# A hybrid decoder layer on one core: modulation blocks loaded ahead of the first weights, and S5's products in turns on the two halves of the rows

## The chip, the core and the metric

One core of a Trainium2 chip runs the whole layer. The metric is the device time of one execution in microseconds (us), as the median of several runs. TensorE (PE, with PEld for its weight loads), VectorE (DVE), ScalarE (ACT), GpSimd (POOL) and SyncE (SP, which issues most of the DMAs) each work through a queue of their own in a fixed order; semaphores hold them back until what they need is there.

## What is computed

The reference takes `x` (1 x 1024 x 1024, float32) and a conditioning vector `c`, and gives an output of x's shape. Cut to what matters here:

```python
cond = silu(c)
mod = cond @ ada_w + ada_b
sh1, sc1, g1, sh2, sc2, g2 = split(mod, 6)
u = rmsnorm(h, norm_mix_w) * (1 + sc1) + sh1
proj = u @ w_in
...
bu = einsum('bsgh,gph->bsgp', ug, bb)
st = associative_scan(combine, (lam, bu))
y = einsum('bsgp,ghp->bsgh', st_re, c_re) - einsum('bsgp,ghp->bsgh', st_im, c_im) + d_skip * u
g = gelu(y)
y_d = g * sigmoid(g @ glu_w + glu_b)
...
h = h + g1 * (groups @ w_out)
v = rmsnorm(h, norm_mlp_w) * (1 + sc2) + sh2
h = h + g2 * (square(relu(v @ mlp_w1)) @ mlp_w2)
out = rmsnorm(h, final_norm_w)
```

The projection `proj` feeds four mixers: a causal pooling, a short gated convolution, an SSD (Mamba-2) and the S5 of the lines above, a state-space model with complex diagonal states in 16 groups.

## The kernel before, in words

The modulation is worked out by DVE, not by PE. The transposed `ada_w` lies in memory as 48 blocks of 128 x 1024, eight for each of the six parts (e = 0 is the shift `sh1`, 1 the scale `sc1`, 2 the gate `g1`, 3 and 4 the second shift and scale, 5 the second gate). `ada_load(e, k)` (L319) loads one, `ada_block` (L324, instruction at L326) multiplies it with the conditioning row and sums each row into a column of `mod`. `modulation` (L335) then makes the columns `amul` (L337) and `ash` (L339) for one block k of 128 input channels.

The input projection begins with the 768 columns that the SSD needs (L601 to L642). The rows of the sequence are taken in two halves h, and in each half k runs over the eight blocks of 128 input channels. In a step, `load_xw(k)` (L577) loads the weights and `split_xw` (L589, L590) splits them into a high part `wh` (on ACT) and a low part `wl` (on DVE), so that three products of the rounded kind make one exact enough. `modulated_T` (L359) transposes four blocks of normalised `x` on PE (L363), scales and shifts them with `amul` and `ash` on ACT (L365, the high part `uh`, and L368, the full one `t_u`) and takes the rest on DVE (L371, the low part `ul`, which it returns). Then 18 products (L638 to L640) add to six banks of PSUM. In the first half each step loads its weights, then two modulation blocks (e = 1 and 0), splits, sums the blocks and calls `modulation`. Before the second half, four more blocks of `x` are loaded (L100) and normalised (`ready`, L568: squares on ACT at L356, L347 and L348 on POOL, the scaling on DVE at L571). In the second half each step sums two more blocks (e = 2 and 4); their loads share three buffers (tag `g5`), while the first half's have four (`m`) and three (`g5`).

`s5_half(b)` (L463) is one half of S5, eight groups in four pairs q; the two groups of a pair, g2 = 0 and 1, lie on rows 0 to 63 and 64 to 127 of the states. After the scans on DVE it has `X[0]` and `X[1]`, the real and imaginary states before each chunk. For each g2 it takes a bank of PSUM, and for each q three products add to a quarter of it: the two states with their tables (L503, L504; 64 rows each, those of g2) and the inputs with a table `T` (L505, all 128 rows). These are plain float32 products, which the trace shows as two instructions each. The GELU follows for each bank on ACT and DVE (L508 to L512), then transposes (L519).

The order of every queue is written by a planner ahead of time. It goes through the program with a clock of its own, and gives each engine the first instruction in the program's order that its clock says is ready; `tc.high_priority()` puts the instructions within it ahead of the rest, and `tc.issue_after(i)` puts those within it behind `i` on i's engine. The chip then runs the queues in that order, whatever the real times are. The small tables of S5 (`s5_small`, L175) come first in the program and fill DVE's queue between other things. `ada_some` (L552) is called after the second half of S5 in program order, and sums eight blocks of e = 3 (`ws_ada`) on DVE, behind the last state of that half.

Of the kernel before, what the change touches and what calls it, by code (L numbers as in the profile page):

```python
# [21 lines left out]
P = 128  # L22
# [29 lines left out]
def body(ctx: ExitStack, tc: tile.TileContext, x, c, pk, adaT, w_x, w_zd, w_pl, w_gl, w_in, w_out, w1, w2, fnw, out):  # L52
    nc = tc.nc
    V, A, PE, G, SY = nc.vector, nc.scalar, nc.tensor, nc.gpsimd, nc.sync
# [14 lines left out]
    def bank(name, tag="ms"):  # L69
        return pp.tile([P, 512], F32, tag=tag, name=name)  # L70
# [25 lines left out]
    xt = [gran(f"x{tb}", tag="x") for tb in range(NB)]  # L96
# [212 lines left out]
    for h in range(2):  # L309
        ps = bank(f"cb{h}", "pj")  # L310
# [8 lines left out]
    def ada_load(s, j, tag="m"):  # L319
        t = gran(f"ada{s}_{j}", tag=tag)  # L320
        lastload[0] = SY.dma_start(out=t, in_=adaT[s * 8 + j])
        return t

    def ada_block(s, j, t):  # L324
        col = mod[:, s * 8 + j:s * 8 + j + 1]
        V.scalar_tensor_tensor(out=t, in0=t, scalar=0.5, in1=cond, op0=MUL, op1=MUL, accum_out=col)  # L326

    amul = small("amul", 8)
    ash = small("ash", 8)
# [5 lines left out]
    def modulation(s_sh, s_sc, j, mulcol, shcol, wname):  # L335
        i, k = s_sc * 8 + j, s_sh * 8 + j
        V.scalar_tensor_tensor(out=mulcol[:, j:j + 1], in0=mod[:, i:i + 1], scalar=adab1[:, i:i + 1],  # L337
                               in1=pv(wname, j, j + 1), op0=ADD, op1=MUL)
        V.tensor_tensor(out=shcol[:, j:j + 1], in0=mod[:, k:k + 1], in1=pv("ada_b", k, k + 1), op=ADD)  # L339
# [19 lines left out]
    def modulated_T(n, k, h, mulcol, shcol, hi, lo, nm, act, t=None):  # L359

        ps = bank(f"tp_{nm}{k}{h}")
        for t4 in range(4):
            PE.transpose(ps[:, t4 * P:(t4 + 1) * P], n[h * 4 + t4][:, k * P:(k + 1) * P], ident)  # L363
        m, b = mulcol[:, k:k + 1], shcol[:, k:k + 1]
        A.activation(out=hi[:, H[h]], in_=ps, func=AF.Identity, scale=m, bias=b)  # L365
        t = t or half(f"t32_{nm}{k}{h}")
        if act:
            A.activation(out=t, in_=ps, func=AF.Identity, scale=m, bias=b)  # L368
        else:
            V.tensor_scalar(out=t, in0=ps, scalar1=m, scalar2=b, op0=MUL, op1=ADD)  # L370
        return V.tensor_tensor(out=lo[:, H[h]], in0=t, in1=f(hi[:, H[h]]), op=SUB)  # L371
# [91 lines left out]
    def s5_half(b, tables, Vb, GT):  # L463

        WT, CP, T, (ct, st) = tables
        ug = lambda g: Vb[:, g * P:(g + 1) * P]
        Zr, Zi, t1, t2 = (half(f"s5{n}{b}") for n in ("zr", "zi", "t1", "t2"))
        pr, pi = bank(f"s5sr{b}"), bank(f"s5si{b}")
        for q in range(4):
            for g2 in range(2):  # L470
                for w_, o in ((WT[0], pr), (WT[1], pi)):
                    PE.matmul(o[64 * g2:64 * g2 + 64, q * P:(q + 1) * P],
                              w_[:, q * P + 64 * g2:q * P + 64 * g2 + 64], ug(2 * q + g2), start=True, stop=True)
        tt(pr, ct, MUL, o=t1)
        tt(pi, st, MUL, o=t2)
        tt(t1, t2, ADD, o=Zr)
        tt(pi, ct, MUL, o=t1)
        tt(pr, st, MUL, o=t2)
        tt(t1, t2, SUB, o=Zi)
        for z in (Zr, Zi):  # L480
            for q in range(4):
                sl = slice(q * P, (q + 1) * P)
                V.tensor_tensor_scan(out=z[:, sl], data0=prm["mag8"][:, 4 * b + q:4 * b + q + 1].to_broadcast([P, P]),
                                     data1=z[:, sl], initial=0.0, op0=MUL, op1=ADD)

        q3 = lambda t: t.rearrange("p (q c) -> p q c", q=4)
        X = [half(f"s5xr{b}"), half(f"s5xi{b}")]
        for xx, a, c_, op in ((X[0], ct, st, SUB), (X[1], st, ct, ADD)):
            V.memset(q3(xx)[:, :, 0:1], 0.0)
            tt(Zr, a, MUL, o=t1)  # L490
            tt(Zi, c_, MUL, o=t2)
            last = V.tensor_tensor(out=q3(xx)[:, :, 1:128], in0=q3(t1)[:, :, 0:127], in1=q3(t2)[:, :, 0:127], op=op)
        Gs = gran(f"s5g{b}", tag="g5")
        c0 = math.sqrt(2.0 / math.pi)
        v8 = lambda t: t.rearrange("p (i e) -> p i e", i=8)

        for g2 in range(2):
            ps = bank(f"s5y{b}{g2}")
            s_ = slice(64 * g2, 64 * g2 + 64)
            for q in range(4):  # L500
                o = ps.rearrange("p (i g e) -> p i g e", i=8, g=4)[:, :, q, :]
                qs = slice(q * P, (q + 1) * P)
                PE.matmul(o, X[0][s_, qs], CP[0][s_, qs], start=True, stop=False)  # L503
                PE.matmul(o, X[1][s_, qs], CP[1][s_, qs], start=False, stop=False)  # L504
                PE.matmul(o, ug(2 * q + g2), T[g2][:, qs], start=False, stop=True)  # L505

            a_, b_ = half(f"s5sq{b}{g2}"), half(f"s5th{b}{g2}")
            A.activation(out=a_, in_=ps, func=AF.Square)  # L508
            V.tensor_scalar(out=a_, in0=a_, scalar1=0.044715 * c0, scalar2=c0, op0=MUL, op1=ADD)
            tt(a_, ps, MUL, o=b_)  # L510
            A.activation(out=b_, in_=b_, func=AF.Tanh)
            V.scalar_tensor_tensor(out=v8(Gs)[:, :, g2 * 64:(g2 + 1) * 64], in0=v8(b_), scalar=1.0, in1=v8(ps),  # L512
                                   op0=ADD, op1=MUL)
        gt3 = GT.rearrange("p (c i) -> p i c", i=8)
        for h in range(2):
            ps = bank(f"s5gp{b}{h}")
            for i4 in range(4):
                i = h * 4 + i4
                PE.transpose(ps[:, i4 * P:(i4 + 1) * P], Gs[:, i * P:(i + 1) * P], ident)  # L519
            A.copy(out=gt3[:, h * 4:(h + 1) * 4, :], in_=ps.rearrange("p (i c) -> p i c", i=4))  # L520
        return last
# [53 lines left out]
    def load_xw(k):  # L575
        t = wp.tile([P, 1024], F32, tag="ws", name=f"ws_x{k}", bufs=2)
        SY.dma_start(out=t[:, 0:768], in_=w_x[k])  # L577
        return t
# [18 lines left out]
    ada_tag = ("m", "g5")  # L597
    uh = [gran(f"uh{k}", F32R, "u") for k in range(NB)] if False else []
    ul = []
    ready(range(4))  # L600
    xb = []  # L601
    for h in range(2):
        if h == 0:
            ps = [bank(f"pjx{i}{h}", "pj" if i < 4 else "ms") for i in range(NX)]
        for k in range(NB):
            if h == 0:
                t = load_xw(k)
                ab = [ada_load(e, k, ada_tag[e]) for e in (1, 0)]
                if k == XAT:
                    with tc.issue_after(lastload[0].ins):  # L610
                        load_x(range(4, NB))
                split_xw(k, t)
                for e in (1, 0):
                    ada_block(e, k, ab[1 - e])
                modulation(0, 1, k, amul, ash, "nw")
                uh.append(gran(f"uh{k}", F32R, "u"))
                ul.append(gran(f"ul{k}", F32R, "u"))
            elif k == 0:
                with tc.issue_after(lastload[0].ins):
                    if XAT >= NB:  # L620
                        load_x(range(4, NB))
                    SY.dma_start(out=pk2, in_=pk[:, first:])
                    plw = small("plw", 256)
                    SY.dma_start(out=plw, in_=w_pl)
                ready(range(4, NB))
            modulated_T(xt, k, h, amul, ash, uh[k], ul[k], "u", True)
            if h == 1 and k == 0:
                for i in range(NX):
                    xb.append(gran(f"xb{i}", tag="x" if i < 4 else "m"))
                    A.copy(out=xb[i][:, H[0]], in_=ps[i])  # L630
                ps = [bank(f"pjx{i}{h}", "pj" if i < 4 else "ms") for i in range(NX)]
            if h == 1:
                for e in (2, 4):
                    ada_block(e, k, ada_load(e, k, "g5"))
            for i in range(NX):
                wh, wl, o = xw_of(k, i)
                c_ = slice(o, o + P)
                PE.matmul(ps[i], wh[:, c_], uh[k][:, H[h]], start=(k == 0), stop=False)  # L638
                PE.matmul(ps[i], wh[:, c_], ul[k][:, H[h]], start=False, stop=False)
                PE.matmul(ps[i], wl[:, c_], uh[k][:, H[h]], start=False, stop=(k == NB - 1))  # L640
# [27 lines left out]
    for b in range(2):  # L668
        ps = proj(8 + b, f"s5{b}")
# [13 lines left out]
    for q in range(8):  # L683
        ps = bank(f"zp{q}", "pj")
        o, ts_ = ps[:, 0:NZ], slice(q * P, (q + 1) * P)
# [78 lines left out]
    ps = bank("sfx")  # L764
# [15 lines left out]
    for q in range(8):  # L780
# [5 lines left out]
        for src, nm in ((ah, "Rh"), (al, "Rl")):  # L786
            o = half(f"{nm}{q}", F32R)
# [717 lines left out]
```

## Time and profile before

| what | value |
|---|---|
| median of three runs | 1042.04 us |
| the runs | 1042.04, 1039.15, 1044.17 us |
| the profiled execution | 1042.58 us |
| its span, first to last instruction | 1040.7 us |
| granted TensorE clock, mean | 0.997 |
| PE busy | 1007.8 us, 97% |
| DVE busy | 767.8 us, 74% |
| ACT busy | 497.9 us, 48% |
| DMA traffic | 175.07 MB, 168 GB/s on average |

The span is what the trace covers, and the profiled execution's own time is 1.9 us longer. A busy PE is not PE at its peak: its instructions overlap, and what counts is the distance from one start to the next. Where an engine sits idle, the profile names the instruction or DMA whose end released it.

### The profile page before, as it was taken

How to read it: one execution, taken by the hardware profiler on the slowest of the kernel's cores; microseconds unless marked ns; L12 is line 12 of the kernel's file. 1: busy time of each engine (PE TensorE's matmuls, PEld its weight loads, DVE VectorE, ACT ScalarE, POOL GpSimd, SP SyncE). 2: the span in 40 equal slices, each digit the busy share in tenths (PEclk: the TensorE clock that was granted, in tenths of full speed). 3: DMA queues.
4: the chain of work that ended last, by engine and by line, in shares of the span. 5: the costliest groups of instructions: out<-in, count | busy, mean ns of one | idle time of the engine just before them, and what ended most of it. 6: DMA issues, size and time to landing. Idle time of an engine off the chain costs nothing.

```text
span 1040.7 us, 13216 instructions
## 1 busy us (share of the span) xinstructions
PE 1007.8 (97%) x4790; PEld 824.7 (79%) x4790; DVE 767.8 (74%) x1361; ACT 497.9 (48%) x825; POOL 48.4 (5%) x80
## 2 busy tenths in 40 slices
PE   4999999999999999999999999999999999999997
PEld 2777897776888888788888888887888888787886
DVE  8999959777788778986667667556644866567884
ACT  5644622315743426765556556564443443433642
POOL 2200000000020112000000000000000000000031
PEclk9999999999999999999999999999999999999999
DMA  9973311125321124145545554378975466787112
GB/s 362 335 259 126 101 45 41 61 64 172 130 114 41 41 75 168 31 152 182 182 163 194 189 186 147 134 300 307 386 280 186 144 200 209 254 305 257 43 52 110
DMA packets 62179, 175.07 MB, mean 168 GB/s; under 512 B 6529, under 2 KB 11137, under 8 KB 62114
## 3 DMA queue, kind: packets, MB, share of 16 engines
q1 hardware_dynamic: 61474, 173.07, 48.1%
q10 hardware_dynamic: 576, 1.05, 0.3%
q8 instruction: 37, 0.61, 0.2%
q14 instruction: 28, 0.23, 0.1%
q0 software_dynamic: 64, 0.11, 0.0%
HBM read 135.17 MB, written 39.04 MB: 167 GB/s over the span
## 4 chain that ended last, share of the span: by engine, by line
PE 77%; DVE 10%; DMA 8%; issue 2%; ACT 2%; POOL 0%; SPq 0%; POOLq 0%; DVEq 0%; ACTq 0%
PE q L1085 6%; PE q L1086 6%; PE q L1084 6%; PE px L1084 5%; PE px L1086 5%; PE px L1085 5%; DMA b12T<-in_w_dram 3%; DMA b21B<-in_w_dram 3%; PE o L959 3%; PE o L960 3%; PE o L961 3%; PE pz L1084 2%; PE pz L1086 2%; PE pz L1085 2%; DVE ada L326 2%; PE pjgh L547 2%
## 5 line engine op out<-in xcount | busy, mean ns | idle before, releaser
L1085 PE MATMUL q<-l_BT,h_AS 128*128 128x512 f32 x192 | 75.2, 392 | 1.2 <-DVE l_BT L1011 1.2
L1086 PE MATMUL q<-h_BT,l_AS 128*128 128x512 f32 x192 | 74.7, 389 | 0.0
L1010 ACT CAST h_AS<-aS 128x1024 fp32r<-128x1024 f32 x32 | 33.6, 1054 | 84.3 <-PE q L1085 69.9
L1084 PE MATMUL q<-h_BT,h_AS 128*128 128x512 f32 x192 | 64.0, 389 | 0.0
L1011 DVE TENSOR_TENSOR woS<-w,woS 128x512 fp32r<-128x512 f32 x60 | 41.2, 691 | 30.7 <-ACT woS L1010 30.7
L1010 ACT CAST woS<-w 128x512 fp32r<-128x512 f32 x60 | 37.2, 624 | 49.7 <-PE px L1086 25.6
L1011 DVE TENSOR_TENSOR l_A<-a,h_A 128x1024 fp32r<-128x1024 f32 x24 | 29.4, 1224 | 38.2 <-ACT h_A L1010 35.1
L1011 DVE TENSOR_TENSOR l_AS<-aS,h_AS 128x1024 fp32r<-128x1024 f32 x32 | 39.0, 1222 | 19.2 <-ACT h_AS L1010 18.9
L959 PE MATMUL o<-wh_wo,yh 128*128 128x512 f32 x128 | 52.5, 410 | 0.1
L960 PE MATMUL o<-wl_wo,yh 128*128 128x512 f32 x128 | 51.8, 405 | 0.0
L961 PE MATMUL o<-wh_wo,yl 128*128 128x512 f32 x128 | 50.8, 401 | 0.0
L1010 ACT CAST h_A<-a 128x1024 fp32r<-128x1024 f32 x24 | 25.2, 1052 | 53.0 <-PE q L1085 44.2
L1085 PE MATMUL q<-l_BB,h_A 128*128 128x512 f32 x128 | 50.0, 391 | 0.5 <-DVE l_BB L1011 0.5
L1086 PE MATMUL q<-h_BB,l_A 128*128 128x512 f32 x128 | 49.8, 389 | 0.0
L138 DVE TENSOR_TENSOR u<-u,pz 128x512 f32<-128x512 f32 x30 | 20.6, 687 | 39.1 <-ACT u L1156 29.0
L1084 PE MATMUL px<-vT,woS 128*128 128x512 f32 x120 | 46.8, 390 | 0.0
L1086 PE MATMUL px<-vT,woS 128*128 128x512 f32 x120 | 46.7, 389 | 0.0
L1085 PE MATMUL px<-vT,woS 128*128 128x512 f32 x120 | 46.7, 389 | 0.0
L966 DVE SCALAR_TENSOR_TENSOR h<-o,br,h 128x512 f32<-128x512 f32 x48 | 35.8, 748 | 11.5 <-PE o L961 11.2
L1085 PEld LDWEIGHTS q<-l_BT,h_AS 128*128 128x128 f32 x192 | 36.0, 188 | 10.2 <-DVE l_BT L1011 2.8
L1084 PE MATMUL q<-h_BB,h_A 128*128 128x512 f32 x128 | 42.6, 390 | 0.6 <-ACT h_BB L1010 0.6
L1010 ACT CAST wo<-w 128x512 fp32r<-128x512 f32 x45 | 27.8, 624 | 30.6 <-PE pz L1086 16.6
(513 smaller groups left out, 2934.0 us busy)
## 6 DMA issues: line engine op xcount, KB each, us to landing
ada<-in_ada_dram SPq DMA_DIRECT2D x32, 512.0 KB, 5.1
aS<-spS SPq DMA_DIRECT2D x32, 512.0 KB, 4.3
w<-in_w_dram SPq DMA_DIRECT2D x30, 512.0 KB, 3.5
spS<-s SPq DMA_DIRECT2D x48, 256.0 KB, 2.2
a<-sp SPq DMA_DIRECT2D x24, 512.0 KB, 5.7
b21B<-in_w_dram SPq DMA_DIRECT2D x16, 512.0 KB, 6.8
b22T<-in_w_dram SPq DMA_DIRECT2D x16, 512.0 KB, 3.6
sp<-u SPq DMA_DIRECT2D x30, 256.0 KB, 2.0
```

The costliest lines, as they stand in the source:

```text
L138: (eng or V).tensor_tensor(out=o, in0=a, in1=b, op=op)
L326: V.scalar_tensor_tensor(out=t, in0=t, scalar=0.5, in1=cond, op0=MUL, op1=MUL, accum_out=col)
L547: PE.matmul(ps[h], w_[:, ks], u_[:, H[h]], start=(a and first), stop=(b and last))
L959: PE.matmul(ps, yh_, wo[b][0][:, H[h]], start=(b == 0), stop=False)
L960: PE.matmul(ps, yh_, wo[b][1][:, H[h]], start=False, stop=False)
L961: PE.matmul(ps, yl_, wo[b][0][:, H[h]], start=False, stop=(b == 1))
L966: V.scalar_tensor_tensor(out=hh, in0=ps, scalar=r[:, tb:tb + 1], in1=hh, op0=MUL, op1=ADD)
L1010: A.copy(out=hi, in_=t)
L1011: return V.tensor_tensor(out=lo, in0=t, in1=f(hi), op=SUB)
L1084: PE.matmul(ps, wh, ub, start=first, stop=False, skip_group_check=more)
L1085: PE.matmul(ps, wh, lb, start=False, stop=False, skip_group_check=more)
L1086: PE.matmul(ps, wl, ub, start=False, stop=last, skip_group_check=more)
```

## The change

In S5 the banks of both g2 are taken first, and for each q the four products of the states come in the order real g2 = 0, real g2 = 1, imaginary 0, imaginary 1, then the two products with `T`. The GELUs follow for both banks. In the projection's first step the two modulation blocks are loaded ahead of the weights; in the other steps the order stays. `modulation` in the first half gets high priority. In the second half, the two blocks of a step are summed on DVE behind that step's `ul` (`lo_`).

```diff
+        banks_ = [bank(f"s5y{b}{g2}") for g2 in range(2)]
+        for q in range(4):
+            qs = slice(q * P, (q + 1) * P)
+            o = [ps.rearrange("p (i g e) -> p i g e", i=8, g=4)[:, :, q, :] for ps in banks_]
+            for r in range(2):
+                for g2 in range(2):
+                    s_ = slice(64 * g2, 64 * g2 + 64)
+                    PE.matmul(o[g2], X[r][s_, qs], CP[r][s_, qs], start=(r == 0), stop=False)
+            for g2 in range(2):
+                PE.matmul(o[g2], ug(2 * q + g2), T[g2][:, qs], start=False, stop=True)
         for g2 in range(2):
-            ps = bank(f"s5y{b}{g2}")
-            s_ = slice(64 * g2, 64 * g2 + 64)
-            for q in range(4):
-                o = ps.rearrange("p (i g e) -> p i g e", i=8, g=4)[:, :, q, :]
-                qs = slice(q * P, (q + 1) * P)
-                PE.matmul(o, X[0][s_, qs], CP[0][s_, qs], start=True, stop=False)
-                PE.matmul(o, X[1][s_, qs], CP[1][s_, qs], start=False, stop=False)
-                PE.matmul(o, ug(2 * q + g2), T[g2][:, qs], start=False, stop=True)
+            ps = banks_[g2]
...
             if h == 0:
+
+                if k == 0:
+                    ab = [ada_load(e, k, ada_tag[e]) for e in (1, 0)]
                 t = load_xw(k)
-                ab = [ada_load(e, k, ada_tag[e]) for e in (1, 0)]
+                if k:
+                    ab = [ada_load(e, k, ada_tag[e]) for e in (1, 0)]
...
-                modulation(0, 1, k, amul, ash, "nw")
+                with tc.high_priority():
+                    modulation(0, 1, k, amul, ash, "nw")
...
-            modulated_T(xt, k, h, amul, ash, uh[k], ul[k], "u", True)
+            lo_ = modulated_T(xt, k, h, amul, ash, uh[k], ul[k], "u", True)
...
             if h == 1:
-                for e in (2, 4):
-                    ada_block(e, k, ada_load(e, k, "g5"))
+                ab = [ada_load(e, k, "g5") for e in (2, 4)]
+                with tc.issue_after(lo_.ins):
+                    for e in (2, 4):
+                        ada_block(e, k, ab[e // 2 - 1])
```

## Rows read from the trace of the kernel before

**Rows 1.** The page's first part: busy time, share of the span, instructions.

```profile
PE 1007.8 (97%) x4790; PEld 824.7 (79%) x4790; DVE 767.8 (74%) x1361; ACT 497.9 (48%) x825; POOL 48.4 (5%) x80
```

**Rows 2.** Busy time by stretch; behind the stretch its length, then each engine.

```profile
core 0: us, PE busy (x) PEld busy (x) DVE busy (x) ACT busy (x) POOL busy (x), PEclk, DMA share, GB/s
0.00:19.16 19.16, 5.64 (x8) 1.88 (x8) 14.45 (x75) 10.01 (x20) 5.74 (x16) 1.00 0.90 345
19.16:49.50 30.34, 30.34 (x139) 25.04 (x139) 30.34 (x110) 18.02 (x33) 6.41 (x7) 1.00 0.97 362
...
120.00:145.00 25.00, 25.00 (x209) 24.57 (x209) 18.59 (x22) 11.68 (x25) 0.00 (x0) 1.00 0.20 66
```

**Rows 3.** Timeline of PE, 0 to 100 us: start, length, instruction, [idle before].

```profile
19.16 2.07 PE L638 MATMUL pjx<-uh,wh_x 128*128 128x512 f32 x4 [4.69 <-ACT uh L365]
...
50.92 0.33 PE L363 MATMUL tp_u<-pkt,x 128*128 128x128 f32 x1 [1.36 <-DVE x L571]
...
69.19 0.50 PE L639 MATMUL pjx<-ul,wh_x 128*128 128x512 f32 x1 [1.69 <-DVE ul L371]
```

**Rows 4.** Timeline of DVE and ACT, 13 to 19 us.

```profile
14.27 1.22 DVE L326 SCALAR_TENSOR_TENSOR ada<-ada,cond 128x1024 f32<-128x1024 f32 x1
14.94 0.40 ACT L589 CAST wh_y<-ws_x 128x256 fp32r<-128x256 f32 x1
16.78 0.22 DVE L337 SCALAR_TENSOR_TENSOR amul<-mod,adab,pkt 128x1 f32<-128x1 f32 x1
...
18.08 0.15 DVE L339 TENSOR_TENSOR ash<-mod,pkt 128x1 f32<-128x1 f32 x1
```

**Rows 5.** The tile of the first weights, 3 to 4.5 us: issue, time to landing.

```profile
L577 SPq DMA_DIRECT2D ws_x<-in_w_x_dram x1: 709/709/709, 3.5 to 3.5; - x1
...
DMA to landing us min/median/max: 7.4/7.4/7.4
```

**Rows 6.** ACT and DVE near 50 us; the loads of x, 33 to 37 us.

```profile
46.05 0.78 ACT L365 ACTIVATE uh<-tp_u,ash,amul 128x512 fp32r<-128x512 f32 x1 [1.73 <-issue]
...
47.39 1.06 ACT L356 ACTIVATE j_u<-x 128x1024 f32<-128x1024 f32 x1
...
50.11 0.75 DVE L571 TENSOR_SCALAR x<-x,rs_u 128x1024 f32<-128x1024 f32 x1 [0.50 <-POOL rs_u L348]
...
L100 SPq DMA_DIRECT2D x<-in_x_dram x4: 422/586/1296, 33.9 to 36.1; - x4
...
DMA to landing us min/median/max: 6.7/7.8/8.3
```

**Rows 7.** Timeline of PE, 173 to 185 us: the first half of S5.

```profile
173.78 0.49 PE L503 MATMUL s5y<-cpr,s5xr 64*128 64x128 f32 x4
...
175.85 0.48 PE L504 MATMUL s5y<-cpi,s5xi 64*128 64x128 f32 x2
...
176.68 0.48 PE L503 MATMUL s5y<-cpr,s5xr 64*128 64x128 f32 x2
177.01 0.38 PE L504 MATMUL s5y<-cpi,s5xi 64*128 64x128 f32 x2
177.32 0.49 PE L505 MATMUL s5y<-toep,s5v 128*128 128x128 f32 x2
177.74 0.48 PE L503 MATMUL s5y<-cpr,s5xr 64*128 64x128 f32 x2
...
183.68 0.71 PE L547 MATMUL pjgc<-uh,wl_gc 128*128 128x512 f32 x2
```

**Rows 8.** Timeline of PE: transposes of full size, products of 64 columns.

```profile
193.77 1.03 PE L519 MATMUL s5gp<-pkt,s5g 128*128 128x128 f32 x8
...
199.38 1.09 PE L472 MATMUL s5sr<-s5v,wTr 128*64 128x128 f32 x16
```

**Rows 9.** Timeline of DVE and PE, 242 to 247 us: the end of S5.

```profile
242.81 1.23 DVE L326 SCALAR_TENSOR_TENSOR ws_ada<-ws_ada,cond 128x1024 f32<-128x1024 f32 x1 [0.27 <-DMA ws_ada<-in_ada_dram]
...
244.93 0.69 DVE L138 TENSOR_TENSOR gq<-gq,pjgh 128x512 f32<-128x512 f32 x1 [0.89 <-PE pjgh L547]
...
246.37 1.06 PE L519 MATMUL s5gp<-pkt,s5g 128*128 128x128 f32 x8 [1.24 <-DVE s5g L512]
```

## The prediction

> **What bounds the kernel now.** I read the page's busy shares first: TensorE (PE) works in 97% of the span [rows 1], so time is won only where PE gets fewer or shorter instructions, or where it stands idle. Then the busy time by stage: PE's idle time is 13.5 us ahead of its first product and little after it; from 19.16 to 49.5 us PE and VectorE (DVE) are both busy without a break and the DMA share is 0.97, so three resources run level there [rows 2]. Third, PE's own order in time: the first product waits until 19.16 us for `uh`, and in the input projection two waits follow, 1.36 us for the normalised `x` and 1.69 us for `ul` [rows 3]. Last, S5's products one by one [rows 7].
>
> The profiled execution took 1042.58 us, 0.54 above the median of the runs, 1042.04; the sum is made against 1042.58. A measurement here can tell about 0.5% from no change, 5.2 us.
>
> **First part: modulation blocks ahead of the first weights.** No instruction is added; on SP the one issue of the first weights (384 KB) moves behind the two of the blocks (512 KB each), and all that follow keep their places; POOL's queue issues none of them. The first weights were issued at 3.5 us and landed 7.4 us later, at 10.9 [rows 5]. At the stage's 362 GB/s [rows 2] the two blocks are worth 2.9 us and the weights 1.1, so the blocks land 1.1 us earlier and the weights at 13.8. On DVE the first block ran at 14.27, after `wl_x` and `wl_y` of step 0; `amul` was made at 16.78, but `ash` only at 18.08, behind both low parts of step 1 [rows 4]. `uh` started when `ash` was done. With the blocks first and the modulation at high priority, both `modulation` instructions stand together: two blocks of 1.22 us each from about 12 us [rows 4], a normalisation of 0.75 [rows 6] between them, 0.3 for the pair: by 15.5 us at the latest. ScalarE (ACT) sets the same time: its casts of step 1 end at 15.3 [rows 4], and the late weights' casts (0.6 and 0.4 us) are in the queue too. Then PE's first product comes at about 16.1 instead of 19.16: 3.1 us at most. In steps 1 to 7 the high priority adds nothing either: the pair, 0.3 us, changes places with low parts that PE needs later than `uh`.
>
> It is not all kept. In the projection PE stops at 50.92 for the last normalised `x` block [rows 3]. That block was issued at 36.1 and landed 6.7 to 8.3 us later; its square stood behind a `uh` with 1.73 us of idle ahead of it and ran at 47.39, and the scaling came at 50.11 [rows 6]. Its transfer can't come earlier, as the DMA engines are full [rows 2]. From the last landing, 44.4 (36.1 + 8.3), a square of 1.06, the 1.66 from its end to the scaling (POOL's part) and the scaling of 0.75 give 47.9. The earlier `ash` takes that `uh` out of the way in part: I put the block at 49.0, between 47.9 and 50.9 and nearer the early end, since the cause of the delay shrinks. PE can keep 50.9 - 49.0 = **1.9 us** (bounds 0 and 3.1).
>
> **Second part: blocks behind `lo_` in the second half.** DVE handles two blocks per step; one was waiting for its DMA with `ul` queued behind it, and PE waited 1.69 us [rows 3]. Now `ul` goes first. Nobody waits for these blocks before the gate row, much later, but their buffers come free later. I take **1.2 us** (bounds: 1.7 gained; the other end is a rival below).
>
> **Third part: S5's products.** The same 24 products per half of S5, each two instructions. Now each group of columns costs 1.06 us per half of the rows: 176.68 to 177.74. In it, from the first 64-row product to the second 0.33, from that to the full-height one 0.31, and 0.42 back to 64 rows [rows 7]. Instructions in one mode follow each other at 0.11 us (eight in 1.03 [rows 8]), so two of them make 0.22, and each change of height costs 0.20. What the two halves of the rows do side by side is in the trace too: at 173.78 the planner had put both halves' first products together, four instructions, and they took 0.49 us; two of one half took 0.48 [rows 7]. Products on the two halves of the columns do it over a longer stretch: 16 instructions in 1.09 us against eight of full size in 1.03 [rows 8].
>
> After the change one group of columns for both halves is: 0.33 + 0.31 for four 64-row products, two and two abreast; 0.42 + 0.22 for the two full-height ones; 1.28 us instead of 2.12. For the first group, whose first products already run together, 0.41 + 0.64 = 1.05 instead of twice 0.83 (175.85 to 176.68). Per half of S5: 3 x 0.84 + 0.61 = 3.1 us. Both banks at once are nothing new: the four instructions at 173.78 write to both. Without overlap the four further 64-row instructions add 0.11 each, 1.72 against 2.12: fewer changes of height alone give 0.4 x 4 = 1.6.
>
> The page "TensorE: Matmul & The Clock Gate" of the Trainium skill (Part 1, on the 56 ns) has a rule against it: without hardware decode the sequencer spends about 62 ns per matmul. By that the eight 64-row instructions would cost 8 x 0.062 + 0.20 = 0.70 instead of 0.64, and the change some 0.4 us less over both halves. The trace speaks for the shorter one: 16 instructions within 1.09 us [rows 8].
>
> In the first half of S5 nothing follows closely: the work queued behind is PE's own, and the casts and copies it waits for are released by PE, so they move along: **3.1 us** (bounds 1.6 and 3.1). In the second half both banks are ready at the same time, and their GELUs no longer lie beside products. There DVE works on the eight `ws_ada` blocks, paced by their loads, ahead of and between the GELU steps; one at 242.81, then a product of `gq` at 244.93 that waits for PE, then `s5g`; PE's transposes started at 246.37 after 1.24 us of idle [rows 9]. If the GELU of the first bank now stands where that of the second stood, `s5g` is made only 0.5 to 1 us earlier than the shift of 3.1 already makes it, and PE waits longer for it. I take **0.9 us** (bounds 0 and 3.1).
>
> Sum: 1.9 + 1.2 + 3.1 + 0.9 = 7.1 us. 1042.58 - 7.1 = 1035.5, and 0.5 less against the median: **1035.0**.
>
> **Rivals.**
> - All is kept: 3.1 + 1.7 + 6.2 = 11.0, 1031.0 against the median. For it: PE is busy 97% [rows 1]. Against it: the full DMA engines [rows 2] and the order around `s5g` [rows 9].
> - Only the first half of S5 is kept: the early start ends at `x`'s wait, DVE (level with PE there, [rows 2]) gives nothing in the second half, `s5g` eats the rest. 3.1 us, 1038.9. For it: the three level resources; against it: DVE idles 6.4 of 25 us in 120 to 145 [rows 2], so a backlog does not last.
> - The change does not do what it says: the planner, which sorts by its own clock, or the array keeps the halves one after the other. Then S5 gives 1.6 once, the start 3.1 at best: 1037.3. Against it: four in 0.49 [rows 7].
> - Slower: the blocks held behind `lo_` free their three buffers one step later, each next load starts later, and in DVE's fixed order a block that waits for it stands ahead of the next step's `ul`. PE then waits the 1.69 us [rows 3] in each of 8 steps: +13.5, less the other 5.9: 1049.6. It decides from about 1.4 us per step on (11.1 / 8). Against it: the change puts each `ul` ahead of its own blocks, and DVE stood idle for DMA only a few times.
>
> **How the numbers follow.** Forecast 0.50 (its own range 1032 to 1038.5), all kept 0.17, only one half 0.20, no overlap 0.05, slower 0.08. Faster by over 0.5% means under 1036.8: 0.38 of the forecast and all of the second, 0.55. Within 0.5%: 0.12 + 0.20 + 0.05 = 0.37. Slower 0.08. The range takes the unknown bounds of both sides, the slower case and the outermost of "all kept" left out: 1029.0 to 1040.5.
>
> **What would show it.** In the profile after: first `pjx` product at about 16 us, with `ash` right behind `amul`; the wait for `x` at about 49 us still there and longer; no wait for `ul` in the second half; an S5 stretch of 4.7 us from the second state product to the next projection instead of 7.8, with eight 64-row instructions in about 0.7 us; the wait ahead of `s5gp` grown from 1.2 to some 3 us. Wrong if the 64-row products of the two halves follow each other, if PE's idle time between 20 and 100 us grows by more than the start won, or if a wait in 250 to 1000 us takes it back.

## The result, and the profile after

The changed kernel takes 1037.62 us (median of 20 runs, 1035.36 to 1040.92); the kernel before, measured beside it, 1043.81 (20 runs). The ratio is 0.9945, with a 95% interval of 0.9935 to 0.9956: 5.7 us less (4.6 to 6.8), where 7.0 was forecast. It is faster by just over 0.5%. The profiled execution took 1036.43 us, with a span of 1034.5 against 1040.7.

First what TensorE waited for `ul` in the input projection, 0 to 100 us, of the changed kernel (tile and line, what was waited for: us in total, times, longest; `...` stands for lines left out, here and below):

```profile
PE pjx L650 <- DVE ul L371: 0.5, 1, 0.5
```

The wait of 1.69 for `ul` in the second half [rows 3] is gone; a new one of 0.51 stands in the first half. Where they are, in PE's timeline after (start, us, and in brackets the idle time ahead of it):

```profile
17.77 2.08 PE L649 MATMUL pjx<-uh,wh_x 128*128 128x512 f32 x4 [2.58 <-ACT uh L365]
...
20.50 1.91 PE L363 MATMUL tp_u<-pkt,x 128*128 128x128 f32 x8
...
23.64 0.39 PE L650 MATMUL pjx<-ul,wh_x 128*128 128x512 f32 x1
...
46.35 0.50 PE L650 MATMUL pjx<-ul,wh_x 128*128 128x512 f32 x1 [0.51 <-DVE ul L371]
...
49.92 0.33 PE L363 MATMUL tp_u<-pkt,x 128*128 128x128 f32 x1 [0.31 <-DVE x L575]
...
64.25 0.72 PE L649 MATMUL pjx<-uh,wh_x 128*128 128x512 f32 x2 [0.43 <-ACT uh L365]
...
170.69 0.49 PE L505 MATMUL s5y<-cpr,s5xr 64*128 64x128 f32 x4
...
172.74 0.49 PE L505 MATMUL s5y<-cpi,s5xi 64*128 64x128 f32 x4
173.16 0.71 PE L507 MATMUL s5y<-toep,s5v 128*128 128x128 f32 x4
173.80 0.49 PE L505 MATMUL s5y<-cpr,s5xr 64*128 64x128 f32 x4
...
174.44 0.71 PE L507 MATMUL s5y<-toep,s5v 128*128 128x128 f32 x4
...
177.49 0.71 PE L551 MATMUL pjgc<-uh,wl_gc 128*128 128x512 f32 x2
...
223.01 0.49 PE L505 MATMUL s5y<-cpr,s5xr 64*128 64x128 f32 x4
...
229.77 0.48 PE L551 MATMUL pjgh<-ul,wh_gh 128*128 128x512 f32 x1
...
234.21 0.61 PE L551 MATMUL pjgh<-uh,wl_gh 128*128 128x512 f32 x2
239.81 1.94 PE L523 MATMUL s5gp<-pkt,s5g 128*128 128x128 f32 x8 [4.98 <-DVE ash L339]
```

The kernel before, for the same places of the projection and of the second half of S5:

```profile
21.89 1.80 PE L363 MATMUL tp_u<-pkt,x 128*128 128x128 f32 x8
...
24.48 0.39 PE L639 MATMUL pjx<-ul,wh_x 128*128 128x512 f32 x1
...
64.83 1.20 PE L638 MATMUL pjx<-uh,wh_x 128*128 128x512 f32 x4 [0.43 <-ACT uh L365]
...
230.48 0.49 PE L503 MATMUL s5y<-cpr,s5xr 64*128 64x128 f32 x4
...
240.33 0.48 PE L547 MATMUL pjgh<-uh,wl_gh 128*128 128x512 f32 x1
```

Read as a lead over the kernel before: the first product 1.4 us (17.77 against 19.16), the third product with `ul` 0.8 (23.64 against 24.48), the first product of the projection's second half 0.6 (64.25 against 64.83), S5's first products 3.1 (170.69 against 173.78), the projection behind S5's first half 6.2 (177.49 against 183.68), S5's second half 7.5 at its beginning and 10.6 at its end, and then only 6.6 at the transposes `s5gp` (239.81 against 246.37 [rows 9]): the wait there grew from 1.24 to 4.98 us. (Its row names `ash`, a short instruction that ends beside the second `s5g`; what the transposes read is `s5g`.) The eight transposes then took 1.94 us instead of 1.06, at half the clock.

The lead at the first product shrank for a reason that the sum left out. Up to about 23 us TensorE ran at half clock in both kernels: eight transposes took 1.91 and 1.80 us there, where eight take 1.03 later [rows 8]. (The 1.00 in the first line of [rows 2] does not show it.) In these two executions the clock rose at nearly the same time, so what was moved ahead of that ran at half speed.

What VectorE did ahead of the transposes `s5gp`:

```profile
232.08 1.22 DVE L326 SCALAR_TENSOR_TENSOR ws_ada<-ws_ada,cond 128x1024 f32<-128x1024 f32 x1 [0.65 <-DMA ws_ada<-in_ada_dram]
...
234.23 1.22 DVE L326 SCALAR_TENSOR_TENSOR ws_ada<-ws_ada,cond 128x1024 f32<-128x1024 f32 x1
...
235.98 0.68 DVE L516 SCALAR_TENSOR_TENSOR s5g<-s5th,s5y 128x512 f32<-128x512 f32 x1
...
236.65 1.27 DVE L138 TENSOR_TENSOR gq<-gq,pjgh 128x512 f32<-128x512 f32 x2
237.84 1.22 DVE L326 SCALAR_TENSOR_TENSOR ws_ada<-ws_ada,cond 128x1024 f32<-128x1024 f32 x1
238.98 0.68 DVE L516 SCALAR_TENSOR_TENSOR s5g<-s5th,s5y 128x512 f32<-128x512 f32 x1
```

Three blocks of 1.22 us and two products of `gq` stand between the GELU steps, and the second `s5g`, for which TensorE waits, comes last.

By stage (stretch, busy us of PE, PEld, DVE, ACT and POOL with their instructions, granted clock, DMA share, GB/s), after:

```profile
176.00:246.00 70.00, 65.02 (x353) 50.62 (x353) 57.23 (x114) 23.09 (x32) 0.00 (x0) 0.95 0.34 106
...
238.34:239.81 1.47, 0.00 (x1) 0.03 (x1) 1.47 (x5) 1.21 (x2) 0.00 (x0) 0.50 0.13 50
239.81:245.16 5.35, 5.35 (x13) 3.28 (x14) 4.67 (x4) 4.61 (x6) 0.00 (x0) 0.50 0.62 196
245.16:247.00 1.84, 1.84 (x8) 1.19 (x7) 0.00 (x0) 0.00 (x0) 0.00 (x0) 1.00 0.48 114
```

The half clock began within the idle time, so it cost less than the mean of 0.95 over 70 us suggests: 5.35 us of work ran at it, some 2.7 us lost. The kernel before had its stretch of half clock elsewhere, behind 24 products of one column in a row (0.43 us from product to product at 290 instead of 0.23 at 289):

```profile
286.23 2.74 PE L851 MATMUL bss<-one,sq 128*128 128x1 f32 x24
...
289.15 0.39 PE L960 MATMUL o<-wl_wo,yh 128*128 128x512 f32 x1
289.38 0.39 PE L961 MATMUL o<-wh_wo,yl 128*128 128x512 f32 x1
...
290.37 0.63 PE L961 MATMUL o<-wh_wo,yl 128*128 128x512 f32 x1
290.80 0.63 PE L959 MATMUL o<-wh_wo,yh 128*128 128x512 f32 x1
```

After, the same 24 products stand in a row (from 281.94 us) and the clock behind them stays whole in this execution:

```profile
281.94 2.74 PE L862 MATMUL bss<-one,sq 128*128 128x1 f32 x24
...
285.09 0.40 PE L972 MATMUL o<-wh_wo,yl 128*128 128x512 f32 x1
285.32 0.39 PE L970 MATMUL o<-wh_wo,yh 128*128 128x512 f32 x1
```

From 300 to 700 us the lead is 5.7, near what these rows add up to: 6.6 at the transposes, less 2.7, and 1.6 back from the kernel before (some eight products at 0.43 instead of 0.23 us), 5.5. At the end it is 6.2.

### The profile page after: what moved, and what is told of

It is laid out like the page before. It is cut to its first block, busy times and chain, and to the rows that moved or that the text cites. A ratio compares the mean times of both kernels' runs of the same rounds, so it can differ in the third digit from the quotient of the medians.

```text
span 1034.5 us, 13214 instructions
## 1 busy us (share of the span) xinstructions
PE 1003.1 (97%) x4790; PEld 821.4 (79%) x4790; DVE 767.5 (74%) x1361; ACT 498.3 (48%) x825; POOL 45.4 (4%) x80
## 4 chain that ended last, share of the span: by engine, by line
PE 78%; DVE 11%; DMA 8%; issue 2%; ACT 1%; POOL 0%; SPq 0%; POOLq 0%; DVEq 0%; ACTq 0%
PE q L1096 7%; PE q L1097 6%; PE q L1095 6%; PE px L1095 5%; PE px L1096 5%; PE px L1097 5%; DMA b12T<-in_w_dram 3%; PE o L970 3%; PE o L971 3%; PE o L972 3%; PE pz L1095 2%; PE pz L1096 2%; PE pz L1097 2%; DMA b21B<-in_w_dram 2%; PE pjgb L551 2%; PE pjpl L551 2%
## 5 line engine op out<-in xcount | busy, mean ns | idle before, releaser
L1096 PEld LDWEIGHTS q<-l_BT,h_AS 128*128 128x128 f32 x192 | 36.0, 188 | 10.6 <-DVE l_BT L1022 3.1
L1095 PEld LDWEIGHTS q<-h_BT,h_AS 128*128 128x128 f32 x192 | 36.0, 188 | 7.5
```

The costliest lines, as they stand in the source:

```text
L1095: PE.matmul(ps, wh, ub, start=first, stop=False, skip_group_check=more)
L1096: PE.matmul(ps, wh, lb, start=False, stop=False, skip_group_check=more)
```

## The experiments

Each was timed in the same session as the kernel before; the differences below are the ratio's, with its interval, against that. The changed kernel's is -5.7 us (-6.8 to -4.6).

**The three parts alone.** Third part:

```diff
+        for q in range(4):
...
+            for r in range(2):
+                for g2 in range(2):
+                    s_ = slice(64 * g2, 64 * g2 + 64)
+                    PE.matmul(o[g2], X[r][s_, qs], CP[r][s_, qs], start=(r == 0), stop=False)
```

> The kernel before with the third part alone (S5's products in turns). Theory (each part gives its own term, and the terms add): the first half of S5 keeps 3.1 us, the second half keeps about 3.1 less the growth of the wait ahead of s5gp (from 1.2 to 3 to 5 us): 3 to 4 us below the kernel before, S5 stretch 4.75 us in each half. Rival (the two halves of S5 are kept whole): 6.2 us below. Rival (the gain of the changed kernel comes from an order of later work that the planner only finds with all parts together): within 1 us of before although both stretches shrink.

Measured: 1040.49 us, -2.7 (-4.0 to -1.6). The stretches shrank as after, the wait grew more than expected:

```profile
245.97 1.30 PE L522 MATMUL s5gp<-pkt,s5g 128*128 128x128 f32 x5 [6.19 <-DVE ash L339]
```

The median lies near the first half's 3.1 us. The second half of S5 kept nothing: in the profiled execution (1042.32 us, one of the slowest of the twelve) the lead was 2.5 us where that half begins (227.96 against 230.48) and 0.4 at the transposes (245.97 against 246.37). First part:

```diff
+                if k == 0:
+                    ab = [ada_load(e, k, ada_tag[e]) for e in (1, 0)]
                 t = load_xw(k)
...
+                with tc.high_priority():
                     modulation(0, 1, k, amul, ash, "nw")
```

> The kernel before with the first part alone (the blocks' loads ahead of the first weights, the modulation at high priority). Theory: as in the changed kernel, the first product 1.4 us earlier and the wait for x 1.0 us shorter, less a new wait of 0.5 for ul: 1.9 us below the kernel before, with the wait of about 1.7 us for ul in the second half of the projection still there. Rival (the early start ends at x's wait, which stays where it was): 0 to 0.5 us.

Measured: 1042.86 us, -0.6 (-1.7 to +0.5). The first product came 1.6 us earlier (17.59) and the wait for `x` shrank to 0.3, but of that 0.7 us is left at the projection's second half (64.08 against 64.83) and 0.6 at S5's first products (173.14 against 173.78). As in the changed kernel, the rest went ahead of 50 us, in products at half clock and in a new wait for `ul` (0.4 of the 2.2 below; 1.3 of it is the old wait of the second half):

```profile
PE pjx L643 <- DVE ul L371: 2.2, 3, 1.3
PE tp_u L363 <- DVE x L571: 0.3, 1, 0.3
```

So this part is worth some 0.6 us, a third of the theory's 1.9. Second part:

```diff
+                ab = [ada_load(e, k, "g5") for e in (2, 4)]
+                with tc.issue_after(lo_.ins):
                     for e in (2, 4):
-                        ada_block(e, k, ada_load(e, k, "g5"))
+                        ada_block(e, k, ab[e // 2 - 1])
```

> The kernel before with the second part alone (in the second half of the projection, the blocks behind the low part of u). Theory: the wait of 1.7 us for ul shrinks to about 0.4; 1.2 us below the kernel before. Rival (the blocks free their buffers later, so that a later step waits): 0 or slower, with a new wait between 60 and 100 us.

Measured: 1039.66 us (6 runs), -3.4 (-4.8 to -2.0): more than the theory's 1.2, which lies outside the interval. No wait for `ul` between 16 and 100 us, none new behind it. The profiled execution began late (first product at 19.92, half clock up to about 26 us) and was 1.2 us behind at the projection's second half, but 1.4 ahead at S5's first products (172.36 against 173.78):

```profile
66.00 1.20 PE L640 MATMUL pjx<-uh,wh_x 128*128 128x512 f32 x4 [0.43 <-ACT uh L365]
```

So the part gained 2.6 us there. The wait that is gone accounts for 1.7; where the other 0.9 comes from is not shown (the order of PE's products changed there as well). Another 1.5 came behind 870 us, where the changed part is long past. Why there is open: the kernels' leads wander by 1 to 3 us behind 700 us in every profile.

The parts sum to -6.7, the whole is -5.7: within the intervals they add.

**What makes the halves quick.** The 64-row products of one half behind those of the other:

```diff
-            for r in range(2):
-                for g2 in range(2):
+            for g2 in range(2):
+                for r in range(2):
```

> The changed kernel with S5's 64-row products of one half of the rows behind those of the other instead of in turns; everything else stands in the same order. Theory (the two halves of the rows work side by side only where they take turns): in each group of columns four of the eight 64-row instructions come at 0.11 us each on top, 1.28 becomes 1.5 to 1.7 us, an S5 stretch 5.7 to 6.5 instead of 4.75; the first half loses 1 to 1.8 us against the changed kernel, the second less, since s5gp waits there anyway. Rival (what counts is only that the height of the tile changes less often): stretches of 4.75 us and the changed kernel's time, 5.7 us below the kernel before.

Measured: 1036.56 us, -4.8 (-6.0 to -3.5), and the stretch is the same:

```profile
173.62 0.50 PE L505 MATMUL s5y<-cpr,s5xr 64*128 64x128 f32 x4
173.94 0.40 PE L505 MATMUL s5y<-cpi,s5xi 64*128 64x128 f32 x4
174.27 0.71 PE L507 MATMUL s5y<-toep,s5v 128*128 128x128 f32 x4
174.91 0.39 PE L505 MATMUL s5y<-cpr,s5xr 64*128 64x128 f32 x2
```

1.29 us per group, as with turns. But the rival's ground does not hold either: eight 64-row instructions take 0.65 us here (173.62 to 174.27) where four took 0.64 before (176.68 to 177.32 [rows 7]), so the halves do run abreast. In the program, and from the second group on in PE's queue as the planner wrote it, `cpi` of one half stands ahead of `cpr` of the other; in the trace all four `cpr` run first. The engine pairs the halves itself: they need only be queued next to each other, without a full-height product between. The Trainium skill speaks otherwise: its page "TensorE: Matmul & The Clock Gate" (Part 3, The mechanism) has products start strictly in program order. These rows differ, and the measurement decides.

Then the changes of height, all full-height products first:

```diff
+        for part in range(2):
             for q in range(4):
...
+                    if part == 0:
+                        PE.matmul(o[g2], ug(2 * q + g2), T[g2][:, qs], start=True, stop=False, skip_group_check=True)
+                    else:
+                        for r in range(2):
+                            PE.matmul(o[g2], X[r][s_, qs], CP[r][s_, qs], start=False, stop=(r == 1), skip_group_check=True)
```

> The changed kernel with S5's full-height products first, for all groups of columns, and then all 64-row products: one stretch of 64-row instructions per half instead of five. Theory (each change of the tile's height costs 0.20 us, and 64-row instructions of the two halves run two abreast at 0.11 us a pair): the 64-row stretch takes 16 x 0.11 + 0.4 = 2.2 us per half, the full-height ones 16 x 0.11 = 1.8 among other products; 4.0 instead of 5.15 us, 1.2 less per half; the first half keeps it, the second ends at the wait for s5gp: 1.2 us below the changed kernel. Rival (a change of height costs nothing by itself, and 64-row instructions in a long row fall out of step): 0 or slower, a 64-row stretch of 3 us and more.

Measured: 1032.11 us, -9.5 (-11.6 to -7.5). In this run each group of columns has a start flag of its own while the other groups of its bank are open, and its sums of S5 lack a part (which products, no run shows). With one flag per bank nothing is left out:

```diff
-                        PE.matmul(o[g2], ug(2 * q + g2), T[g2][:, qs], start=True, stop=False, skip_group_check=True)
+                        PE.matmul(o[g2], ug(2 * q + g2), T[g2][:, qs], start=(q == 0), stop=False, skip_group_check=True)
```

> S5's full-height products first, as in the run before, with the start flag on the first product of each bank alone, so that every group of columns keeps its whole sum. Theory (the flag costs no time; the gain comes from the height changes left out and from the shorter wait ahead of s5gp): the time of the run before, 9 to 10 us below the kernel before and about 4 below the changed kernel. Rival (that run lay low by the scatter of executions): 5.7 to 7.5 below the kernel before.

Measured: 1032.97 us, -9.7 (-11.6 to -7.7), so the flag costs no time, and this is the best kernel here (the last one below can't be told from it): its interval and the changed kernel's don't meet. Its timeline of PE:

```profile
158.88 0.60 PE L504 MATMUL s5y<-toep,s5v 128*128 128x128 f32 x4
159.84 1.58 PE L504 MATMUL s5y<-toep,s5v 128*128 128x128 f32 x12 [0.35 <-DMA toep<-kpad]
...
172.85 0.49 PE L507 MATMUL s5y<-cpr,s5xr 64*128 64x128 f32 x4
...
174.94 0.73 PE L551 MATMUL pjgc<-uh,wh_gc 128*128 128x512 f32 x2
...
176.03 0.73 PE L551 MATMUL pjgc<-uh,wl_gc 128*128 128x512 f32 x2
...
236.18 1.94 PE L523 MATMUL s5gp<-pkt,s5g 128*128 128x128 f32 x8 [3.38 <-DVE s5g L516]
```

The 32 64-row instructions take 2.09 us, within 0.1 of the 2.2 expected. At the same product of the projection it leads the changed kernel by 1.5 us (176.03 against 177.49; 1.2 expected; a wait of 0.43 for `wh_gc` is gone and one of 0.35 for `toep` has come), at `s5gp` by 3.6 (236.18 against 239.81), because the second half's banks are ready earlier and the wait is 3.38 instead of 4.98. So the second half is not all eaten, against what I expected. "TensorEngine Tiling (Array Packing)" of the Trainium skill (Key Properties) says that a change of tiling mode drains the engine, without a figure. The trace does not show the drain itself, but a cost that fits it: 0.20 us per change of height.

**What makes the wait ahead of `s5gp`.** Three places for the eight blocks. First, one behind each output weight: the call of eight is left out, and the calls that stand there anyway take the blocks.

```diff
-    with tc.issue_after(last.ins):
-        ada_some(8)
```

> The changed kernel without the call that handles eight modulation blocks right behind S5's state chain: one follows each of the eight output weights instead. Theory (the wait of 4.98 us ahead of s5gp is made by these blocks standing on VectorE ahead of and between the GELU steps, and the half clock behind it by that idle time): the wait falls to under 1 us, the transposes take 1.0 us instead of 1.9, the clock between 176 and 246 us is 1.00; 5 to 8 us below the changed kernel, so 11 to 14 below the kernel before. Rival (the GELU's own chain over two banks that are ready at the same time is the wait): the wait stays over 3 us and the time within 2 us of the changed kernel. Rival (the blocks only move their cost into 250 to 330 us, where VectorE then is late): the wait goes, and the time stays.

Measured: 1042.36 us, -1.1 (-2.5 to +0.3): 4.6 us slower than the changed kernel, although the wait ahead of `s5gp` is gone. The blocks are not the only reason: the planner also put 32 products of the projection `pjgb` ahead of the transposes, which start at 241.93, 2.1 us later than in the changed kernel. PE now waits 4.2 us for the last output of the state-space scan (`sdt` for `btk`). Second, behind the GELU and behind the last gated weights:

```diff
-            V.scalar_tensor_tensor(out=v8(Gs)[:, :, g2 * 64:(g2 + 1) * 64], in0=v8(b_), scalar=1.0, in1=v8(ps),
+            last_g = V.scalar_tensor_tensor(out=v8(Gs)[:, :, g2 * 64:(g2 + 1) * 64], in0=v8(b_), scalar=1.0, in1=v8(ps),
...
-        return last
+        return last_g if b else last
...
-    with tc.issue_after(last.ins):
-        ada_some(8)
...
         yb.append(y)
+    with tc.issue_after(last.ins):
+        ada_some(8)
```

> The changed kernel with the eight modulation blocks behind the last GELU step of S5 and behind the loads of the last gated pair's weights; they then stand at 240 to 260 us, where VectorE worked only 3.95 us of 14. Theory (the blocks on VectorE make the wait of 4.98 us ahead of s5gp, and the half clock follows from that idle time): the wait is under 1 us, the clock between 176 and 246 us is 1.00, no new wait of more than 1 us up to 400 us; 5 to 7 us below the changed kernel, 11 to 13 below the kernel before. Rival (what the blocks cost there is paid later, as where they were spread over the output weights): waits of 3 us and more between 260 and 400 us, and a time within 2 us of the changed kernel. Rival (the half clock comes back at the one-column products near 285 us): the wait goes, 1.5 to 3 us of the gain are lost there.

Measured: 1038.11 us, -3.3 (-4.7 to -2.0), no gain. Waits of PE from 176 to 400 us, and two stretches:

```profile
PE sdt L851 <- DVE btk L849: 4.1, 1, 4.1
```

```profile
176.00:246.00 70.00, 70.00 (x391) 55.64 (x388) 51.72 (x99) 23.14 (x32) 0.00 (x0) 1.00 0.25 75
...
260.00:290.00 30.00, 30.00 (x159) 26.08 (x158) 27.31 (x44) 19.55 (x45) 5.86 (x4) 0.89 0.54 198
290.00:400.00 110.00, 104.82 (x537) 86.56 (x536) 84.61 (x151) 42.05 (x108) 11.79 (x27) 0.95 0.19 67
```

PE works 70.00 of the 70 us around `s5gp`, at the full clock. Here too 32 products of `pjgb` fill the place (the transposes start at 242.32), so the missing wait alone proves nothing; `s5g` was done at 237.65 us instead of 239.66. But the scan, a chain of eight chunks, began at 259.9 us (its first `sdd` triple) against 259.1 in the changed kernel, and gave its last output at 376.55 against 375.0. PE had run its other work sooner and waited 4.1 us for it, with two stretches of half clock. Over the six runs the mean clock was 0.992, over the changed kernel's 0.994; 0.002 of 1037 us is worth about 2.2 us, nearly all of the 2.4 by which this kernel is behind. Third, behind the GELU but ahead of the last gated weights, so that the order puts the scan's first chunks earlier:

```diff
-            V.scalar_tensor_tensor(out=v8(Gs)[:, :, g2 * 64:(g2 + 1) * 64], in0=v8(b_), scalar=1.0, in1=v8(ps),
+            last_g = V.scalar_tensor_tensor(out=v8(Gs)[:, :, g2 * 64:(g2 + 1) * 64], in0=v8(b_), scalar=1.0, in1=v8(ps),
...
-        return last
+        return last_g if b else last
```

> The changed kernel with the eight blocks behind the last GELU step of S5, still ahead of the last gated pair's weights; TensorE's order then has the gate row and the first two chunks of the state-space scan ahead of the last gated projection. Theory (what was lost when the blocks were moved later is the scan: it runs some 116 us from its first decay product to its last output in every kernel, and its start at 259 us sets when the last 96 output products can run): the scan starts at 250 us or earlier, its last output comes at 368 or earlier instead of 375, no wait of 4 us for it; 3 to 7 us below the changed kernel, 9 to 13 below the kernel before. Rival (the last gated projection now waits for its weights behind the eight blocks): a wait of 3 us or more at its first product, a time within 2 us of the changed kernel.

Measured: 1036.17 us, -5.3 (-7.1 to -3.6), the changed kernel's time. The transposes ran at 235.25 without a wait, behind the same products as in the changed kernel: this shows that the blocks made the wait. The scan began at 246.6, but it took 122.9 us (last output 369.5) where the changed kernel's took 115.9, with waits of its own:

```profile
235.25 1.04 PE L523 MATMUL s5gp<-pkt,s5g 128*128 128x128 f32 x8
```

```profile
PE sy L830 <- DVE dec L138: 2.3, 1, 2.3
```

Neither theory nor rival: the gated projection did not wait; the scan did, on VectorE, which had the blocks to do in its first chunks. The clock was 0.88 from 246 to 260 us, behind the first of those waits, and 0.97 from 290 to 400, where the changed kernel had 1.00 in both. (The scan's 116 us "in every kernel" is no constant either: in the kernel before it took 119.9.) The same on top of the best kernel (that edit with the one before):

> The same with the eight blocks behind the last GELU step, in place. Theory (what was left of the wait ahead of s5gp, 3.4 us, was made by the blocks, and the scan starts earlier): the wait is under 1 us, 10 to 13 us below the kernel before. Rival (as without the new order of the products, the wait comes back as waits of the scan): 8 to 10 below, with a wait of 2 us or more at the scan's products.

Measured: 1033.39 us, -10.0 (-11.8 to -8.3), where theory and rival meet; its waits are the rival's. The one ahead of `s5gp` is gone, one of 2.8 us at `sy` has come.

**The start.** The low part of the first weights put behind the shift `ash` in VectorE's order:

```diff
+                    sh_ = modulation(0, 1, k, amul, ash, "nw")
+                if not k:
+                    split_xw(k, t, sh_)
...
+            with tc.issue_after(after.ins) if after else contextlib.nullcontext():
+                V.tensor_tensor(out=lo, in0=src, in1=f(hi), op=SUB)
```

> The changed kernel with the low part of the first weights put behind the shift of the modulation in the order of VectorE. Theory (the first product came at 17.8 instead of 16.1 us because that low part still stood ahead of the shift, and because the second block is handled behind a normalisation): first product at 16.9 to 17.2, some 0.6 to 0.9 us earlier, and the time 0 to 0.9 below the changed kernel, the wait for x near 50 us growing by what is not kept. Rival (the first product waits for its weights' cast or for the transposes): no earlier than 17.7.

Measured: 1037.56 us, -3.7 (-5.0 to -2.4), nothing won. `ash` now ran at 16.32 ahead of `wl_x`, and the first product at 17.40, 0.4 earlier and not 0.6 to 0.9. Behind it PE waited for `ul` twice, 1.0 us in all instead of 0.5, and at 100 us it was no further than the changed kernel. With both this edit and the blocks behind the GELU:

> The changed kernel with both of the last two edits: the blocks behind the GELU and the shift ahead of the first low part. Theory: their gains add, 5 to 8 us below the changed kernel. Rival: the planner's order of later work changes with either, and the sum is off by more than 1.5 us.

Measured: 1038.86 us, -2.1 (-3.4 to -0.8): no gains to add.

## Why the prediction was right, and where it was not

The sign, the range and the sum held: 7.1 forecast, 6.2 between the two profiles, 5.7 by the ratio. That the sum held is in part luck: the first term was too large by 1.3 us and the second too small by 1.3, and of the 2.7 by which the last term failed, 1.8 were won elsewhere. By its terms:

- **Start, 1.9: wrong, 0.6.** The first product came at 17.77, not 16.1. The first step that failed: "both `modulation` instructions stand together ... by 15.5 us at the latest". The second block stood behind the normalisation and `amul` and ended at 15.93, `wl_x` still went ahead of `ash` in spite of the high priority, and `ash` came at 16.69. The second: "PE can keep 50.9 - 49.0 = 1.9". The block of `x` came 1.0 us earlier (49.92), and PE was no earlier than before when it got there: of its 1.4 us, 0.6 had gone in products at half clock ahead of 23 us, and most of the rest in the new wait for `ul` at 46.35. So the wait for `x`, said to be longer, shrank from 1.36 to 0.31, and 0.6 us is left at 64 us. Undoing the first failed step gave 0.4 us at the first product and nothing at the end: `ul` is the next limit.
- **Blocks behind `lo_`, 1.2: too small, 2.5.** The lead grew from 0.6 at 64 us to 3.1 at S5's first products, and by 2.6 where this part stood alone; its bound was 1.7. The wait of 1.69 is gone whole (the 0.43 at 64.25 is in the kernel before too, at 64.83); the other 0.8 no wait shows. The slower rival (blocks that wait for buffers, in each step) did not show at all.
- **S5, first half, 3.1: right.** 4.75 us from 172.74 to 177.49 against 7.83; 1.29 per group against 1.28 forecast. Eight 64-row instructions took 0.64 us (173.80 to 174.44). By the rule of "TensorE: Matmul & The Clock Gate" in the Trainium skill (Part 1, on the 56 ns), some 62 ns per matmul with hardware decode off, they would have taken 0.70, by the prediction's estimate; the trace does not show that floor, and no run shows which decode was on.
- **S5, second half, 0.9: wrong, it lost.** The stretch shrank as much as the first, to 4.75, but the step "PE waits longer for it", from 1.2 to some 3 us, was too small: 4.98 us. And it left out the clock: TensorE went on at half clock behind that idle time, some 2.7 us lost. Of a lead of 10.6 at the end of S5, 5.7 are left at 300 us, and that with about 1.6 us back, because the half clock behind the one-column products (0.43 for 0.23 us over some eight products) did not come after. Against the lead of 7.5 at this half's beginning that is a loss of 1.8.
- What makes up for it was not in the sum: the wait of 0.61 for `wh_gh` between the halves is gone, other products changed places (together 1.3 us between 177 and 223), and 0.5 came behind 700 us.

The rival "only the first half of S5 is kept" named the right mechanism for the second half, `s5g` behind VectorE's blocks, and was nearly right on the start, but gave up the second part, which brought 2.5. That the blocks make the wait is shown where they alone were moved behind the GELU and PE's products ahead of the transposes stayed (e5_blocks_in_place, and e14_full_first_gelu beside e13_full_first_once). That this would win the 5 us is refuted: the scan's waits and longer stretches of half clock took them.

## What to carry over

Products on separate row halves run abreast when nothing of another height stands between them, so group by height first: full-height products in one row and half-height ones in another won more here (about 4 us beyond the change, at least 0.9 by the intervals) than taking turns. When a change makes two results ready at once, count what the engine that handles them has queued between their steps; and before moving that work, find the serial chain downstream that will meet it. And read a lead again some way behind the place where it was won: 1.4 us at the first product were 0.6 at 64 us.

## What the runs showed that was not expected

- The engine does not keep to program order between the two row halves: with the halves one behind the other in the program, their instructions ran paired, 1.29 us per group either way. What is said further up, that the chip runs the queues in the planner's order, does not hold between the halves.
- TensorE's half clock is not where one order puts it. It came behind 4.98 us of idle time in the changed kernel, and behind 24 one-column products in the kernel before. The run without turns has the changed kernel's order but for S5, and there both came (granted clock 0.95 from 176 to 246 us and 0.96 from 246 to 290, where the changed kernel had 1.00). In twelve of the fourteen traces a stretch of half clock begins during or behind these products, near 270 to 290 us; not in the changed kernel's and not in e1_s5_only's. Over the runs of the changed kernel the mean clock lay between 0.991 and 0.996, with a mean of 0.994 where the kernel before had 0.996 (beside the first four experiments). From its 20 runs, 0.005 of clock is some 5 us, which is the spread of their times (1035.4 to 1040.9).
- A high priority given to two short instructions did not bring the second ahead of a low part that the plan had first.
